# One wait of the store queue, moved up by one store, in a row-sum kernel on one Trainium2 core

## The chip, the core and the metric

The kernel runs on one core of a Trainium2 chip. A core has compute engines that run side by side, each through its own list of instructions in order. Two of them compute here: VectorE (DVE in the profile) and ScalarE (ACT). SyncE (SP, and SPq in the profile for its issuing instructions) computes nothing: it issues all DMA transfers and waits on semaphores between them. The engines meet only through semaphores, which compute instructions raise by 1 and DMA transfers by 16 in all. The metric is the time of one execution on the device in microseconds (us), the median of three runs.

## The reference: what is computed

```python
def setup_inputs():
    batch, seq, dim = 32, 512, 1024
    return {"x": np.random.randn(batch, seq, dim).astype(np.float32)}

def reference(x):
    relu_x = np.maximum(x, 0)
    return np.sum(relu_x, axis=-1).astype(np.float32)
```

Each of the 32 x 512 = 16,384 rows of 1,024 floats is clipped at zero and summed. 67.11 MB are read, 64 KB are written.

## The kernel before

**Tiling.** The rows are dealt to the 128 partitions, 128 rows to each. Of the output they form three regions, `REGIONS = [1, 111, 16]` rows per partition. In the first region, partition p holds row p. In the second, each partition holds 111 rows that follow one another, and in the third 16. The sums are gathered in `res`, 128 partitions by 128 columns, one column for each row of a partition.

**Loads.** Seven chunks of 16 rows per partition (8 MB each) go to three buffers in turn. SP issues them at line 91; from the fourth chunk on it first waits until DVE is done with the buffer (`s_dve`, lines 86 and 87). Then follow, with no wait between them but the one on the first, the loads of the last region: 8, 4 and 2 rows (line 101), and the last two rows in four pieces. Three pieces are issued at line 112, with one semaphore each, `s_in[-3]`, `s_in[-2]` and `s_in[-1]`. The third piece, 256 columns, is the last load but one. The fourth, `seam` (line 115, semaphore `s_seam`), takes the rest, 368 columns across the border between the two rows, and is the last load.

**Compute.** In the first six chunks ACT clips (line 145) and DVE sums (line 160). From the seventh chunk on, each engine clips and sums whole rows by itself, every other one (helpers at lines 127 and 130). Of the last two rows, DVE sums the third piece when `s_in[-1]` is there (lines 197 and 198), and both engines finish on `seam` (lines 201 and 203), which raises `s_last` to 2.

**The first region's sums.** They stand in column 0 of `res`, one float in each partition. After chunk 1, DVE transposes the first 32 columns in blocks of 32 by 32 into `turned` (line 169) and raises `s_turn`. The sums are then in the four partitions 0, 32, 64 and 96, 32 floats (128 bytes) in each.

**Stores.** All three are issued by SP, in this order, after all loads:

1. line 117: the 4 x 128 bytes of `turned`, after a wait for `s_turn` (line 116). This text calls it the turned store.
2. line 123: the second region, 128 partitions x 444 bytes (55.5 KB), after waits for the last sums of that region (`s_fact`, `s_fdve`, lines 120 and 121) and for `s_in[-1]` (line 122). This is the bulk store. Both of these raise `s_store` by 16.
3. line 207: the third region, 128 x 64 bytes (8 KB), after a wait for `s_last` (line 206). This is the final store; it raises `s_out`.

The program ends when `s_store` stands at 32 and `s_out` at 16 (lines 208 and 209). A wait need not become an instruction of its own: one wait rides on the DMA instruction behind it, and others are put together in one wait instruction ahead of it. In the trace, SP has a single wait instruction ahead of the bulk store (for `s_in[-1]` and `s_fdve`, shown as line 122), and the bulk store itself carries the wait for `s_fact`.

Of the kernel before, what the change touches and what calls it, by code (L numbers as in the profile page):

```python
# [16 lines left out]
def bass_relu_sum_kernel(  # L17
# [40 lines left out]
    s_in = [nc.alloc_semaphore(f"s_in{i}") for i in range(n_in)]  # L58
# [11 lines left out]
    sp, act, dve = nc.sync, nc.scalar, nc.vector  # L70
# [40 lines left out]
    for k, (lo, hi) in enumerate((first, second, third)):  # L111
# [2 lines left out]
        )  # L114
    sp.dma_start(out=seam[:, 2 : 2 + w + HEAD], in_=rows[:, CUT : D + HEAD]).then_inc(s_seam, 16)
    sp.wait_ge(s_turn, 1)
    sp.dma_start(
        out=of[0:P].rearrange("(k q) -> k q", q=32), in_=turned[0:P:32, 0:32]
    ).then_inc(s_store, 16)
    sp.wait_ge(s_fact, 1)  # L120
    sp.wait_ge(s_fdve, 1)
    sp.wait_ge(s_in[-1], 16)
    sp.dma_start(out=ov[1][:, :], in_=res[:, start[1] : start[2]]).then_inc(s_store, 16)


# [112 lines left out]
```

## Time and profile before

| | |
|---|---|
| median of 3 runs | 160.82 us (160.79 to 160.82) |
| span of the profiled execution, first to last instruction | 159.4 us (159.394 in the trace) |
| what lies around the span, by the difference to the median | 1.43 us |
| DVE busy | 120.6 us, 76% of the span |
| ACT busy | 101.5 us, 64% of the span |
| DMA queue | 2,456 packets, 67.18 MB, 98.1% of 16 engines' span |
| mean rate of reading HBM | 421 GB/s |

No separate total time is recorded for the profiled execution, so its span stands beside the median of the timed runs. Times below that count from the start of the span are points on the trace's clock.

The profile page gives each engine's busy time, a chain of work that ended last, and groups of instructions with their mean durations. The trace behind it holds every instruction with its start and duration, every DMA packet, and the time of every increment that reached a semaphore. A view of waits tells what an engine waited for, and a view of stretches gives the busy time and the moved bytes between two points.

### The profile page before, as it was taken

What the parts mean: (1) busy time and instruction counts of PE and PEld (TensorE: products, weight loads), DVE (VectorE), ACT (ScalarE), POOL (GpSimd) and SP (SyncE); (2) the same over time, 40 slices, a digit from 0 to 9 for tenths busy, and PEclk for the clock granted to TensorE, in tenths of its full rate; (3) what the DMA queues carried; (4) which work ended last, traced back from release to release, by engine and by line L of the source; (5) the groups of instructions that cost most, each with busy time, mean ns of one, the idle gap of its engine ahead of it and who ended that gap; (6) DMA issues with size and microseconds to landing.
All of it is one profiled execution on the core that took longest, in us unless ns stands there. A gap on an engine that the chain in (4) does not pass through costs nothing.

```text
span 159.4 us, 150 instructions
## 1 busy us (share of the span) xinstructions
DVE 120.6 (76%) x59; ACT 101.5 (64%) x54; POOL 0.2 (0%) x4
## 2 busy tenths in 40 slices
DVE  0000000009999999999999999999999999898995
ACT  3000059980799708996099941999329980496975
POOL 0000000000000000000000000000000000000000
DMA  9997996996996997989979969969969979798994
GB/s 378 493 401 339 493 526 263 526 526 263 526 493 296 526 444 345 526 378 411 526 312 477 526 263 526 526 263 526 526 263 526 444 345 526 321 469 374 417 400 142
DMA packets 2457, 67.18 MB, mean 421 GB/s; under 512 B 536, under 2 KB 792, under 8 KB 1176
## 3 DMA queue, kind: packets, MB, share of 16 engines
q1 hardware_dynamic: 2456, 67.18, 98.1%
q14 instruction: 1, 0.01, 0.0%
HBM read 67.11 MB, written 0.07 MB: 421 GB/s over the span
## 4 chain that ended last, share of the span: by engine, by line
DVE 55%; DMA 34%; ACT 9%; SPq 2%; issue 0%
DVE res L160 54%; DMA buf<-in_x_dram 34%; ACT buf L145 9%; SPq L101 1%; SPq L112 1%; DVE buf L130 0%; DVE seam L130 0%; SPq L91 0%; DVE turned L169 0%
## 5 line engine op out<-in xcount | busy, mean ns | idle before, releaser
L160 DVE TENSOR_REDUCE res<-buf 128x4 f32<-128x4096 f32 (+3 forms) x18 | 99.4, 5596 | 35.5 <-ACT buf L145 35.5
L145 ACT ACTIVATE buf<-buf 128x7168 f32<-128x7168 f32 (+5 forms) x13 | 80.4, 6233 | 46.1 <-DMA buf<-in_x_dram 46.1
L127 ACT ACTIVATE buf<-buf 128x1024 f32<-128x1024 f32 (+2 forms) x19 | 19.0, 999 | 8.9 <-DMA buf<-in_x_dram 8.9
L130 DVE TENSOR_SCALAR_CACHE_REDUCE buf<-buf 128x1024 f32<-128x1024 f32 (+2 forms) x19 | 20.7, 1143 | 1.7 <-DMA buf<-in_x_dram 1.6
L127 ACT ACTIVATION_READ_ACCUMULATOR buf<-buf 128x1 f32 x19 | 3.6, 188 | 0.0
L145 ACT ACT_TABLE_LOAD x1 | 1.3, 1283 | 1.3 <-PEq L223 1.3
L130 DVE DVE_READ_ACCUMULATOR buf<-buf 128x1 f32 x19 | 1.6, 84 | 0.0
L130 DVE TENSOR_SCALAR_CACHE_REDUCE seam<-seam 128x258 f32<-128x258 f32 x1 | 0.4, 421 | 0.0
L127 ACT ACTIVATE seam<-seam 128x114 f32<-128x114 f32 x1 | 0.3, 300 | 0.1
L169 DVE STREAM_TRANSPOSE turned<-res 128x32 f32<-128x32 f32 x1 | 0.2, 211 | 0.0
L127 ACT ACTIVATION_READ_ACCUMULATOR seam<-seam 128x1 f32 x1 | 0.2, 186 | 0.0
L223 POOL MEMSET const-bfloat16-1.0<- 128x1 bf16 x1 | 0.1, 101 | 0.0
L223 POOL MEMSET const-uint8-127<- 128x1 uint8 x1 | 0.1, 101 | 0.0
L223 POOL MEMSET const-float32-0.0<- 128x1 f32 x1 | 0.1, 98 | 0.2 <-issue 0.2
L223 POOL MEMSET const-float32-1.0<- 128x1 f32 x1 | 0.1, 98 | 0.0
L130 DVE DVE_READ_ACCUMULATOR seam<-seam 128x1 f32 x1 | 0.1, 82 | 0.0
## 6 DMA issues: line engine op xcount, KB each, us to landing
buf<-in_x_dram SPq DMA_DIRECT2D x1, 7680.0 KB, 21.1
buf<-in_x_dram SPq DMA_DIRECT2D x1, 4096.0 KB, 25.3
buf<-in_x_dram SPq DMA_DIRECT2D x1, 2048.0 KB, 29.9
buf<-in_x_dram SPq DMA_DIRECT2D x1, 1024.0 KB, 31.9
buf<-in_x_dram SPq DMA_DIRECT2D x1, 512.0 KB, 3.3
buf<-in_x_dram SPq DMA_DIRECT2D x1, 456.0 KB, 32.5
buf<-in_x_dram SPq DMA_DIRECT2D x1, 256.0 KB, 32.7
seam<-in_x_dram SPq DMA_DIRECT2D x1, 184.0 KB, 32.6
```

The costliest lines, as they stand in the source:

```text
L101: sp.dma_start(out=buf[:, tb, r : r + n, :], in_=xv[-1][:, r : r + n, :]).then_inc(s_in[NBIG + i], 16)
L112: sp.dma_start(out=flat[:, lo:hi], in_=rows[:, lo:hi]).then_inc(s_in[NBIG + len(TAIL) + k], 16)
L127: return act.activation(t, t, AF.Relu, accum_out=acc)
L130: return dve.tensor_scalar(out=t, in0=t, scalar1=0.0, scalar2=None, op0=ALU.max, op1=ALU.add, accum_out=acc)
L145: act.activation(t, t, AF.Relu).then_inc(s_act, 1)
L160: dve.tensor_reduce(out=res[:, c * BIG + r : c * BIG + r + n], in_=buf[:, c % NB, r : r + n, :], axis=X, op=ALU.add,).then_inc(s_dve, 1)
L169: dve.transpose(out=turned[:, :], in_=res[:, 0:32]).then_inc(s_turn, 1)
L223: nc = _bacc.Bacc("TRN2", target_bir_lowering=False, num_devices=1)
```

## The change

```diff
     sp.dma_start(out=seam[:, 2 : 2 + w + HEAD], in_=rows[:, CUT : D + HEAD]).then_inc(s_seam, 16)
     sp.wait_ge(s_turn, 1)
+    sp.wait_ge(s_in[-1], 16)
     sp.dma_start(
         out=of[0:P].rearrange("(k q) -> k q", q=32), in_=turned[0:P:32, 0:32]
     ).then_inc(s_store, 16)
     sp.wait_ge(s_fact, 1)
     sp.wait_ge(s_fdve, 1)
-    sp.wait_ge(s_in[-1], 16)
     sp.dma_start(out=ov[1][:, :], in_=res[:, start[1] : start[2]]).then_inc(s_store, 16)
```

The wait for `s_in[-1]` moves from the bulk store to the turned store in front of it. SP issues the same three stores in the same order. The turned store is now issued after the last load but one has landed, and the bulk store is issued after the turned store, its own waits for `s_fact` and `s_fdve` between them. Nothing changes on DVE and ACT, nor in the loads.

## The prediction

> **What bounds the kernel now.** I read the page's head and its chain first, then the end of the chain in order of time, then SP's waits, because the change touches only SP.
>
> ```profile
> span 159.4 us, 150 instructions
> ...
> q1 hardware_dynamic: 2456, 67.18, 98.1%
> ...
> DVE 55%; DMA 34%; ACT 9%; SPq 2%; issue 0%
> ```
>
> The DMA engines are full for 98% of the span: the kernel is bound by reading its input. Nothing in the diff touches that stream until it runs dry, so the question is the last three microseconds. The chain of work in order of time ends so (start, length, what):
>
> ```profile
> 124.39 32.60 DMA buf<-in_x_dram
> 156.99 0.02 issue
> 157.01 0.44 DVE buf L130 x2
> 157.45 0.02 issue
> 157.47 0.43 DVE seam L130 x2
> ```
>
> The third piece of the last rows lands at 156.99 (`s_in[-1]`). DVE sums it, then the seam, and is done at 157.90. The rest is stores. SP's timeline (start, length) and its waits (total, times, longest) show where:
>
> ```profile
> 124.87 0.44 SPq L115 DMA_DIRECT2D seam<-in_x_dram  x1
> 125.35 0.63 SPq L117 DMA_DIRECT2D out_dram<-turned  x1
> 157.08 0.34 SPq L123 DMA_DIRECT2D out_dram<-res  x1
> 157.93 0.34 SPq L207 DMA_DIRECT2D out_dram<-res  x1
> ```
>
> ```profile
> SPq L122 <- DMA buf<-in_x_dram: 31.0, 1, 31.0
> ...
> SPq L209 <- DMA out_dram<-res: 1.1, 1, 1.1
> SPq L207 <- DVE seam L130: 0.5, 1, 0.5
> ```
>
> The turned store's issue stands at 125.35, in a gap of 31 us in which SP has nothing else to do. The bulk store follows 156.99 at once. Then SP idles 0.51 us (157.42 to 157.93) until DVE is done, and issues the final store. It idles 1.1 us more until that lands. So the tail now has two spare places: **0.51 us of SP** between the two stores, and the distance between the bulk store's landing and the final store's. The trace's record of semaphore arrivals gives the second. The bulk store's 16 increments come in two groups, 13 at 158.47 to 158.70 and three stragglers at 159.02, 159.03 and 159.05. The final store's come at 159.17 to 159.35. So the bulk store has **0.30 us** to spare. Counted from the issue's start the bulk store lands after 1.39 to 1.97 us (from 157.08), the final one after 1.24 to 1.42 us (from 157.93). The view of stretches (columns: stretch, length, busy times, clock, DMA share, GB/s) shows the same gap from issue to movement:
>
> ```profile
> 157.00:157.90 0.90, 0.85 (x4) 0.76 (x4) 0.00 (x0) 1.00 0.00 0
> 157.90:158.30 0.40, 0.00 (x1) 0.00 (x0) 0.00 (x0) 1.00 0.50 142
> 158.30:158.75 0.45, 0.00 (x0) 0.00 (x0) 0.00 (x0) 1.00 0.00 0
> 158.75:159.00 0.25, 0.00 (x0) 0.00 (x0) 0.00 (x0) 1.00 0.37 33
> ```
>
> The bulk store's bytes move from 157.92 on, 0.84 us behind its issue, the final store's from 158.76, 0.83 us behind its own, and between them nothing moves.
>
> **The change part by part.**
>
> *Removed: the turned store in the 31 us gap.* Its 0.63 us of issue were hidden there and give back nothing. Its four packets lay behind the loads: by the packet records they ran at 156.53 to 156.63, 13 ns each, and their increments came at 157.15 to 157.32. They stand behind the seam's packets, so I take the gain for the loads as 0. The other bound is in the last rival.
>
> *Added: the turned store between 156.99 and the bulk store.* What it costs SP there isn't in the trace. Its own row says 0.633 us, but that was the last of eight issues in a row. In that row, issues behind another take 0.433 to 0.463 us, and issues after a wait 0.327 to 0.343. The turned store has 0.633 - 0.441 = 0.192 us more than the load just before it. After a wait I therefore take 0.343 + 0.192 = **0.535 us**; bounds 0.34 (an issue like any other after a wait) and 0.63 (its own row).
>
> *Added: one wait instruction.* Before, the two waits that remained ahead of the bulk store rode in one wait instruction and on the store. Now each of the two stores has two waits, so a wait instruction stands between them as well. Both its semaphores were raised by 146.94 (their arrivals), so it costs only its passing: the start of SP's wait instruction to the start of the bulk store was 0.075 us, and one issue's end to the next start 0.042 us, together **0.12 us**; the lower bound is 0.04, if it vanishes.
>
> *Moved: the bulk store.* It starts 0.535 + 0.12 = 0.655 us later, at 157.735 (bounds 0.38 and 0.75 later). Its landing moves with it: 159.05 + 0.655 = 159.705. The 0.30 us to spare are used up and **0.355 us** stay over.
>
> *Moved: the final store.* Queued behind the bulk store on SP. The bulk issue takes 0.343 us (after a wait) to 0.441 us (behind another issue), so SP is free at 158.08 to 158.18 and starts the final store 0.042 us later, at 158.12 to 158.22 instead of 157.93. That is 0.19 to 0.29 us late, and with 1.42 us to landing the end is 159.54 to 159.64. This is less than the 0.355 of the bulk store. The two run side by side, so the larger counts.
>
> *The rest.* The turned store itself lands early enough: with even the bulk store's longest 1.97 us it is there at 159.05. No load, ACT or DVE instruction waits for any of SP's stores.
>
> **The sum**: 159.394 + 0.355 = 159.75 us of span; around it stay 1.43 us, so 160.82 + 0.355 = **161.17 us**, 0.22% more. A change of 0.2%, 0.32 us, is about what a measurement of this kernel can tell from none; the forecast is just beyond it.
>
> *Two rules weighed.* The record of arrivals for the turned store shows five: one at 126.37, 0.39 us behind the end of its issue, and four with its packets. The Trainium skill, DMA: Bandwidth & Descriptors, section on why a DMA increments its semaphore by 16, says that a transfer which uses only k engines has the issuing sequencer write the other 16 - k itself, at once; that fits the 0.192 us more on the issue, and by it that surcharge goes along to the new place. The same page (Rules for kernel authors) says to issue a DMA early so that its fixed cost overlaps, which speaks against this change, and its section on the anatomy of one DMA puts that fixed cost at about 2.0 us (for another issuing path). By that price a bulk store at 157.735 would land at 159.74 and the final store at 160.12, which would make the loss 0.77 us; but the same price makes the final store of before land at 159.93, and its row says 159.35, so the rows decide.
>
> **The rivals.**
>
> 1. *The stragglers don't come again.* If the three late arrivals of the bulk store belong to that one execution, its landing is 158.70 + 0.655 = 159.36 and the final store decides: +0.19 to +0.29, so 161.01 to 161.11 us, within 0.2%. For it: 13 of 16 arrivals come 0.3 us sooner. Against it: the bulk store's 128 packets of 444 bytes are the same after the change.
> 2. *The spare SP time swallows nearly all* (the side of not slower). Place: the 0.51 us of SP before the final store; price: if the turned store costs only 0.34 + 0.04 us after a wait, the bulk store starts at 157.46, its issue ends at 157.80, and the final store stays at 157.93. The bulk landing is 159.43, +0.08, so 160.90 us. It decides as long as the bulk store is delayed less than 0.47 us (0.51 less one gap), for then the final store doesn't move. For it: after waits all of SP's issues fall to 0.33 to 0.34. Against it: the 0.192 us surcharge over a load beside it.
> 3. *SP is held until the early increment has arrived.* That was 1.02 us behind the start of the issue (126.37 against 125.35). No DMA was issued behind it before, so the trace can't exclude it. Then the bulk store starts at about 157.08 + 1.02 + 0.08 = 158.18, 1.10 us later, and lands at 160.15: +0.80, 161.62 us. Against it: SP's wait instruction counts its 31.0 us from 125.99, the end of the issue.
> 4. *The loads gain by the store's removal.* In the last 3 us of loading (154 to 157) the rates are 391, 383 and 265 GB/s in the three stretches of 1 us, 1.04 MB; at the mean 421 GB/s that takes 2.47 us instead of 2.96, so 0.49 us is the most that undisturbed reads could give. With rival 2's +0.08 that is 160.41 us; it becomes faster than 0.2% only if both hold. Against it: the four packets ran at 156.53, after 2.5 of those 3 us.
>
> **How the numbers follow.** Forecast 0.46: its range 161.05 to 161.30, of which 0.38 lies beyond 161.14. Rival 1: 0.20. Rival 2: 0.11. Rival 3: 0.16. Rival 4: 0.07. Slower by over 0.2%: 0.38 + 0.16 = 0.54. Within 0.2%: 0.08 + 0.20 + 0.11 = 0.39. Faster: 0.07. The range takes in rivals 1 and 2 at the low end (160.88) and the larger part of rival 3's way at the high end (161.55). What it leaves out is rival 4 and the end of rival 3.
>
> **What would show it.** In the changed profile: L117 (one line lower) starts at about 157.08 and takes 0.53 us; a wait instruction and the bulk store's issue follow at 157.7; the final store's issue starts at 158.1 to 158.2 without a wait for DVE ahead of it; the chain ends through SP, not DVE; the bulk store's last increment comes at 159.7, at or behind the final store's. `s_in[-1]` still lands at 156.99. I'm wrong in the first step if the turned issue takes 0.34 or over 0.7 us, in the second if the bulk arrivals have no stragglers, and altogether if the last load lands earlier or later by more than 0.1 us.

## The result and the profile after

The changed kernel takes **162.29 us** (162.19 to 162.33), the kernel before 160.82 (160.79 to 160.87): a ratio of **1.0089**, 95% interval 1.0077 to 1.0101. It is slower by 1.47 us, as forecast in sign, but four times the forecast 0.35, and outside the range. The span grew by more, 1.57 us (159.39 to 160.96): around it lie 1.37 us here, where the prediction took 1.43 from a median and a span of different executions.

The profiled execution took 162.33 us, 160.96 us of it span. The head of the page after:

```profile
span 161.0 us, 151 instructions
...
DVE 120.6 (75%) x59; ACT 101.5 (63%) x54; POOL 0.2 (0%) x4
...
q1 hardware_dynamic: 2456, 67.18, 97.1%
q14 instruction: 1, 0.01, 0.0%
```

The engines' work is the same to a tenth. SP has one instruction more. SP's waits after (total, times, longest) and its timeline in the tail:

```profile
SPq L117 <- DMA buf<-in_x_dram: 31.7, 1, 31.7
...
SPq L209 <- DMA out_dram<-res: 2.2, 1, 2.2
```

```profile
157.15 0.63 SPq L118 DMA_DIRECT2D out_dram<-turned  x1
157.89 0.35 SPq L123 DMA_DIRECT2D out_dram<-res  x1
158.29 0.42 SPq L207 DMA_DIRECT2D out_dram<-res  x1
```

The 0.5 us wait for DVE ahead of the final store is gone, as said, and the final store is issued 0.36 us later. But the last wait is 2.2 us instead of 1.1. The issues' view of the same kernel (size, us from issue to landing) gives for the final store

```profile
out_dram<-res SPq DMA_DIRECT2D x1, 8.0 KB, 2.6
```

where the kernel before has

```profile
out_dram<-res SPq DMA_DIRECT2D x1, 8.0 KB, 1.4
```

This is the row that the prediction didn't see coming: the same 8 KB take 1.2 us longer to land. The view of stretches, after (stretch, length, busy times, clock, DMA share, GB/s), shows when they move:

```profile
159.20:159.42 0.22, 0.00 (x0) 0.00 (x0) 0.00 (x0) 1.00 0.39 35
159.42:159.57 0.15, 0.00 (x0) 0.00 (x0) 0.00 (x0) 1.00 0.00 0
159.57:159.94 0.37, 0.00 (x0) 0.00 (x0) 0.00 (x0) 1.00 0.07 24
159.94:160.90 0.96, 0.00 (x0) 0.00 (x0) 0.00 (x0) 1.00 0.00 0
```

The final store's packets run from 159.21, and 120 of its 128 are through at 159.41. Then something runs from 159.57 to 159.94 that fills only 0.07 of the engines, one of 16, at 24 GB/s. The packet records name it: one packet of 8,192 bytes on **queue 14**, the `q14 instruction` of the page, from 159.571 to 159.878; and behind it, from 159.875 to 159.924 (their starts), the last eight of the final store's packets, as many as one DMA engine's share. What kept them from 159.21 until the fetch's packet began, at 159.571, stands in no record. Fifteen of the final store's increments had come by 160.04. The sixteenth came at **160.92**, and the span ends on it. Before, this same instruction fetch stood behind all stores (final store's packets, nothing, the fetch):

```profile
158.76:158.97 0.21, 0.00 (x0) 0.00 (x0) 0.00 (x0) 1.00 0.44 39
158.97:159.21 0.24, 0.00 (x0) 0.00 (x0) 0.00 (x0) 1.00 0.00 0
159.21:159.39 0.18, 0.00 (x0) 0.00 (x0) 0.00 (x0) 1.00 0.17 46
```

### The profile page after: what moved, and what is told of

It is laid out like the page before. It is cut to its first block, busy times and chain, and to the rows that moved or that the text cites. A ratio compares the mean times of both kernels' runs of the same rounds, so it can differ in the third digit from the quotient of the medians.

```text
span 161.0 us, 151 instructions
## 1 busy us (share of the span) xinstructions
DVE 120.6 (75%) x59; ACT 101.5 (63%) x54; POOL 0.2 (0%) x4
## 4 chain that ended last, share of the span: by engine, by line
DVE 54%; DMA 33%; ACT 9%; SPq 2%; issue 0%
DVE res L160 54%; DMA buf<-in_x_dram 33%; ACT buf L145 9%; SPq L101 1%; SPq L112 1%; DVE buf L130 0%; DVE seam L130 0%; SPq L91 0%; DVE turned L169 0%
## 6 DMA issues: line engine op xcount, KB each, us to landing
buf<-in_x_dram SPq DMA_DIRECT2D x1, 456.0 KB, 32.6
seam<-in_x_dram SPq DMA_DIRECT2D x1, 184.0 KB, 32.6
```

## The experiments

**The theories.** A: the final store, now late, meets the instruction fetch; one DMA engine carries its share behind the fetch, and that increment, alone 0.88 us behind the others, is most of the loss. The variants of A differ in what sets off the fetch. B: the writes of three stores in flight hold each other up, and the fetch is incidental. C: it needs the turned store's four packets or its issue.

### Seven runs that repeated the two kernels

I wanted to move the fetch by lengthening one engine's instruction stream with no-operations, 64 of them or one, and in e11 to delay the final store with 18:

```diff
+    for _ in range(64):
+        nc.vector.nop(nofuse=True)   # DVE; in other runs SP, ACT, POOL, PE
     k = 0
     for c in range(NTWO):
```

The traces don't have the no-operations: each engine has as many instructions there as without them, and in e11 the final store is issued at 158.286, where the changed kernel has 158.293. I take it that they never reached the chip. So these runs tell nothing of what they were made for, and are repeats: six of the changed kernel, one of the kernel before.

> The changed kernel with 64 no-operation instructions on SP in its idle 31 us, ahead of the turned store's waits. Theory A (the 8 KB instruction fetch seen at 159.571, on queue 14, holds up one DMA engine's share of the final store; it comes when SP reaches a certain place in its instruction stream): the no-operations move the fetch away from the tail, the last increment at 160.92 goes, the rest ends as the other 15 do at 160.04, so 161.4 us. Theory B (the final store is late because three stores' writes are in flight together; the fetch only happens to be there): 162.3 us.

> The kernel before with a single no-operation on SP in the idle 31 us, so that its stream has as many instructions as the changed kernel's. Theory A, if the place is a count of instructions: the fetch comes one instruction sooner and can meet the final store, up to 161.9 us. Theory A, if the fetch is tied to the final store's own issue, and theory B: 160.8 us.

> The changed kernel with 64 no-operations at the head of DVE's stream, where DVE idles until 35 us. The no-operations on SP left the fetch where it was, so SP's stream isn't what fetches. Theory A2 (the fetch belongs to the stream of another engine that comes to its end at about 157.9): on the engine that owns it the no-operations move it out of the tail, and the time falls to 161.2 to 161.5 us; on the other engines nothing moves, 162.3. DVE is my first guess. Theory B (stores' writes hold each other up): 162.3 us on all four engines.

> The same on ACT, which idles until 21 us. Theory A2: 161.2 to 161.5 us if the fetch is ACT's, my second guess, 162.3 otherwise. Theory B: 162.3 us.

> The same on GpSimd (POOL), which has nothing to do after its four memsets. Theory A2: 162.3 us, since its stream comes to its end early, unless it waits for the others at the end and fetches there: then 161.2 to 161.5. Theory B: 162.3 us.

> The same on TensorE (PE), which has nothing to do in this kernel. Theory A2: 162.3 us, since its stream comes to its end early, unless it waits for the others at the end and fetches there: then 161.2 to 161.5. Theory B: 162.3 us.

> The changed kernel with 18 no-operations on SP ahead of the final store's wait, so that it is issued later still, by some 0.3 to 0.9 us (what a no-operation costs on SP isn't known from the runs so far). Theory A: packets that come after the fetch has ended (159.9) aren't held up, so the time hardly rises or falls in spite of the delay: 161.8 to 162.4 us, and the 16 increments come close together. Theory B and a plain delay: 162.3 plus the whole delay, 162.6 to 163.2.

Measured: 162.35, 162.23, 162.30, 162.32, 162.32 and 162.32 us for the six (in the order above without the second), and 160.81 us for e2. As repeats they show that the picture is no accident. In all six profiles the last of the final store's packets starts 0.045 or 0.046 us after the fetch's packet has ended, and one increment is alone, 0.89 to 1.14 us behind the other fifteen. In e2, as before, the packets are through ahead of the fetch.

### e3, e4 and e10: is it the turned store, or the lateness?

e3 issues the bulk store first and the turned store between it and the final one:

```diff
-    sp.wait_ge(s_turn, 1)
-    sp.dma_start(... in_=turned[0:P:32, 0:32]).then_inc(s_store, 16)
     sp.wait_ge(s_fact, 1)
     sp.wait_ge(s_fdve, 1)
     sp.wait_ge(s_in[-1], 16)
     sp.dma_start(out=ov[1][:, :], in_=res[:, start[1] : start[2]]).then_inc(s_store, 16)
+    sp.wait_ge(s_turn, 1)
+    sp.dma_start(... in_=turned[0:P:32, 0:32]).then_inc(s_store, 16)
```

> The order bulk store (with the wait for the last load but one), turned store, final store; SP has as many instructions as before. The bulk store stays at 157.08, the final store is issued behind the turned store at about 158.1. Theory A: its packets come later after its issue than behind a wait (0.92 us instead of 0.83) and can meet the fetch, 162.0 us or, where the fetch stays behind, 161.0. Theory B: three stores in flight, 162.0 us. My prediction's account, in which stores only queue on SP: 161.0 us.

e4 is the changed kernel with one semaphore for the two waits ahead of the bulk store, so that the wait instruction between the stores goes:

```diff
-    sp.wait_ge(s_fact, 1)
-    sp.wait_ge(s_fdve, 1)
+    sp.wait_ge(s_fact, 2)
```

> The changed kernel with one semaphore in place of s_fact and s_fdve, so that the wait instruction between the turned and the bulk store goes and SP has as many instructions as before. Theory A, if the place is a count of instructions: the fetch comes one instruction later and misses the final store, 161.3 us. Theory A tied to the final store's issue: 162.2 us. Theory B: 162.2 us (0.05 less for the wait instruction).

e10 is the kernel before, the turned store early, with another wait ahead of the bulk store:

```diff
-    sp.wait_ge(s_in[-1], 16)
+    sp.wait_ge(s_last, 2)
     sp.dma_start(out=ov[1][:, :], in_=res[:, start[1] : start[2]]).then_inc(s_store, 16)
```

> The kernel before, the turned store early as it was; the bulk store waits for s_last instead of the last load but one, so that bulk and final store are issued one behind the other from 157.93 and the final store at about 158.31. Theory A: its packets run at 159.2 and one engine's share meets the fetch, 162.2 us. Theory C (it needs the turned store in the tail, its four packets or its longer issue): 161.2 us. Theory B: between them, two stores in flight instead of three, 161.3 to 161.8.

Measured: e3 162.09, e4 162.35, e10 162.19 us (ratio of e10 to before 1.0083, 1.0068 to 1.0098). SP's timeline of e10 and the landing of its final store:

```profile
158.18 0.34 SPq L123 DMA_DIRECT2D out_dram<-res  x1
158.56 0.43 SPq L207 DMA_DIRECT2D out_dram<-res  x1
```

```profile
out_dram<-res SPq DMA_DIRECT2D x1, 8.0 KB, 2.2
```

In e10 no turned store is near; its packets are there at 156.5, with the loads. Still one increment of the final store comes alone, at 160.76, the others by 160.17, and the fetch lies at 159.414 to 159.776. So C falls: **a late final store is enough**. e3 says the same with the bulk store at its old place (fetch 159.343 to 159.723, last increment 160.69; its time fits A and B alike). e4 shows that the number of SP's instructions doesn't set off the fetch: with one less, it comes at 159.570, against 159.571.

### e13 and e9: moving the fetch by an engine's end

In both, the changed kernel gets one op more on one engine, behind its last sum, into a spare cell; no store waits for it. e13 on ACT, e9 on DVE:

```diff
     on_dve(seam[:, k : k + HEAD + 2], res[:, J - 1 : J]).then_inc(s_last, 1)
+    on_act(flat[:, D + D // 2 : 2 * D], spare[:, 1:2])    # e13
+    on_dve(flat[:, CUT // 2 : CUT], spare[:, 0:1])        # e9, instead
```

> The same with ACT in place of DVE: one op more (512 elements) after its last sum, so that only ACT's end comes 0.8 us later. Theory A3: 161.3 us if the fetch is ACT's, otherwise 162.3. Theory B: 162.3 us.

> The changed kernel; DVE does one op more (456 elements of a piece that is already summed, into a spare cell) after its last sum has raised s_last, so that only DVE's end comes 0.7 us later. No store waits for it. Theory A3 (the fetch comes at the end of one engine's own work, about 1.3 to 1.5 us behind it): if the engine is DVE, the fetch moves to about 160.2, behind the final store's packets, and the time falls to 161.3 us; if not, 162.3. Theory B (stores' writes hold each other up): 162.3 us.

Measured: **e13 161.33 us** (ratio to before 1.0032, 1.0021 to 1.0044), as the theory had it for the owner of the fetch; **e9 161.90 us** (1.0069, 1.0054 to 1.0084), neither of its two numbers. A useless op on ACT takes 0.96 us off the changed kernel. The stretches and the final store's row of e13 show why:

```profile
159.20:159.42 0.22, 0.00 (x0) 0.00 (x0) 0.00 (x0) 1.00 0.34 29
159.42:159.85 0.43, 0.00 (x0) 0.00 (x0) 0.00 (x0) 1.00 0.00 0
159.85:159.93 0.08, 0.00 (x0) 0.00 (x0) 0.00 (x0) 1.00 0.59 102
```

```profile
out_dram<-res SPq DMA_DIRECT2D x1, 8.0 KB, 1.6
```

The three stores are issued at 157.11, 157.85 and 158.24, within 0.05 us of the changed kernel's, with the same writes in flight. But the fetch now comes at 159.857, behind the final store's packets (159.161 to 159.359), and all 16 increments are there by 159.89. **So B falls, and the collision's price is 0.96 us** (1.03 us of span). e13 also has a second fetch, at 161.228, behind the span; with ACT's two instructions more it may be ACT's, but no run tells. Of all eighteen profiles, ten have the final store's lone late increment, and in these ten and no others its last eight packets start at the fetch's end, 3 to 4 ns ahead of it.

In e9 there is no fetch in the tail either, and the final store's increments stay together. But the fetch has moved the other way, to 151.616 among the loads, and the last load but one lands at 157.64, its other fifteen increments by 157.09. The same holds for every load that lands behind the fetch, there and in e18 below: one increment comes 0.54 to 0.66 us behind the others, where the loads ahead of the fetch have at most 0.1.

### e15, e16, e18: whose fetch it is

e15 (on the changed kernel) and e16 (on the one before) sum pieces that are ready together in one op, five DVE instructions fewer for the same work:

```diff
-DVE_STEPS = [[4, 5, 7], [7, 4, 5], [7, 4, 5], [7, 4, 5], [4, 5, 7], [3, 4, 5]]
+DVE_STEPS = [[16], [7, 9], [7, 9], [7, 9], [4, 5, 7], [3, 4, 5]]
```

e18 is e9's op on the kernel before.

> The changed kernel with five instructions fewer on DVE: in the first four chunks, pieces that are ready at the same time are summed in one op instead of two or three. Theory A4 (the fetch is DVE's, and comes when DVE's stream reaches a certain count just behind its last sum, past the wait at the program's end): with five instructions fewer that count is reached only after the stores have landed, no fetch lies in the span, and the time is 161.2 to 161.4 us. If the fetch is ACT's or anyone else's, and theory B (the stores hold each other up): 162.2 to 162.3 us.

> The same five instructions fewer in the kernel before. Theory A4: no fetch in the span, but there it was behind the final store's packets and cost nothing, 160.7 to 160.85 us. If the fetch also made the three late increments of the bulk store, these go, without effect on the end.

> The kernel before with one DVE op more behind its last sum (nothing waits for it). Theory A4: as in the changed kernel with this op, the fetch comes at about 151.6 among the loads, one DMA engine's share of every later load comes about 0.5 us late, and the time is 161.3 to 161.5 us. If that late load in the changed kernel was chance, 160.8 us.

Measured: e15 161.80 us (1.0057, 1.0042 to 1.0072), e16 161.33 us (1.0032, 1.0019 to 1.0045), e18 161.47 us (1.0038, 1.0023 to 1.0053). The queues on the page of e15:

```profile
q1 hardware_dynamic: 2456, 67.18, 97.7%
HBM read 67.11 MB, written 0.07 MB: 420 GB/s over the span
```

The line for q14 is gone: no fetch in the span, which falls to 159.93 us, 1.03 less than after. That is the expected mechanism. The expected time isn't met, in e15 nor in e16: the fetch still comes, at 161.608 and 161.145, behind the span, in what the program does after its last instruction, and that is longer. Between total and span of the same execution lie 1.85 us in e15 (161.78 - 159.93) and 1.89 in e16 (161.34 - 159.45), against 1.37 in the changed kernel. e16's span is as before, 159.45. That the fetch makes this half microsecond is argued from its place, not shown: in both runs the semaphore signals of the program's end stand still 0.42 us longer than elsewhere, but they go on 0.31 and 0.35 us before the fetch's packet has ended, and e13, which has a packet of that kind behind its span too, has 1.49.

e18 met its range. The fetch is at 151.707, and the end of its chain of waits (start, length, what) and the row of the last load but one (us to landing) read:

```profile
124.48 33.24 DMA buf<-in_x_dram
157.73 0.02 issue
```

```profile
buf<-in_x_dram SPq DMA_DIRECT2D x1, 128.0 KB, 33.2
```

against 32.60 and 32.6 before. Fifteen of its increments are there by 157.16, the last at 157.73: one engine is late, and every sum behind it. So adding DVE instructions, before or after, draws the fetch forward by over seven microseconds, and removing them pushes it back by two, while ACT's two in e13 move it by 0.29: **its place goes by DVE's instructions**, so I take the fetch for DVE's. That ACT's op also moved it, while DVE's own end stayed, fits a wait of DVE for ACT at the program's end: a semaphore that the kernel doesn't use is raised there three times, the last at 158.06 before and at 158.70 in e13, and the fetch follows 1.15 and 1.16 us behind. It isn't a fixed distance: in the changed kernel the fetch comes 1.43 us behind (158.14), and 1.18 to 1.47 in the other nine runs where it meets the final store. This link is argued, not shown; e13 met its number, while e9, on the engine that I take for the owner, missed. Why two instructions more move the fetch by seven microseconds stays open.

### e17: a shorter way to the final store

The changed kernel, with the first region's sums stored from 128 partitions, 4 bytes each:

```diff
     sp.dma_start(
-        out=of[0:P].rearrange("(k q) -> k q", q=32), in_=turned[0:P:32, 0:32]
+        out=ov[0][:, :], in_=res[:, 0:1]
     ).then_inc(s_store, 16)
```

> The changed kernel; the first region's sums are stored from all 128 partitions, 4 bytes each out of res, in place of 128 bytes from each of four. Its issue should take 0.34 to 0.44 us instead of 0.63, so the final store is issued at about 158.0 to 158.1 and its packets run from 158.9 to 159.1. Theory A: if they are through before the fetch at 159.2, 160.95 to 161.1 us; if some are not, 162.0. Theory B: 161.9 us or more, 128 more small writes being in flight.

Measured: 167.68 us (1.0429, 1.0412 to 1.0445). The issue took 0.343 us, the final store's issue started at 157.96, and its packets ran from 158.89 to 159.10, ahead of the fetch (159.345), all about as expected. The time was missed by over 6 us. The landings of the three stores (bulk, turned, final):

```profile
out_dram<-res SPq DMA_DIRECT2D x1, 55.5 KB, 8.3
out_dram<-res SPq DMA_DIRECT2D x1, 0.5 KB, 5.9
out_dram<-res SPq DMA_DIRECT2D x1, 8.0 KB, 8.2
```

512 bytes in writes of 4 take 5.9 us to land and hold up the stores behind them to 8 us, although the last packet of all three is through at 159.10. (The first two raise one semaphore; the view gives its first sixteen increments to the first, so 5.9 us is the least.) The run can't tell how much lateness the collision needs; it says what the transpose on DVE is there for.

No version beat the kernel before. Its fetch has the best place that the runs show.

## Why the prediction was wrong

**Right: the removal.** Nothing was gained at 125 us, and the loads gained nothing, though the turned store's packets had run among the seam's (to 156.97) and not behind them: the last load but one landed at 157.07, against 156.99. Rival 4 falls.

**Right in kind, too small: the turned store's issue.** 0.632 us after a wait, not 0.535. It is its own row of before, the upper bound. e17's 0.343 for the same place with 128 partitions shows the surcharge: 0.29, not 0.192. The increment that came ahead of the packets is there again 1.01 us behind the issue's start (158.16); SP wasn't held until it, so rival 3 falls.

**Right: the wait instruction and SP's queue.** From the end of the turned issue to the bulk's start 0.108 us (forecast 0.12); the bulk's issue took 0.349; the final issue started 0.36 us later than before, of which 0.08 is the loads' later end. The forecast was 0.19 to 0.29.

**Wrong: which store lands last.** The bulk store's three stragglers didn't come again. Its last increment came at 159.53, 1.64 us behind its start, not 1.97. This was rival 1, and with it the final store decides. e2, the repeat of the kernel before, has no stragglers either: its bulk store is there at 158.72, 0.65 us ahead of the final store's 159.37. So the 0.30 us to spare, on which the forecast's 0.355 stands, was a reading of one execution. In e13 six of the bulk's increments come in a late group again, at 159.58 to 159.67, so the stragglers come and go; what makes them stays open.

**The step that failed: "Moved: the final store", with "1.42 us to landing".** I carried the landing time along as a constant of the transfer. It was 2.62 us (158.293 to 160.917). e13 splits the difference. Without the collision the final store is issued 0.31 us later than before (158.24) and takes 1.65 us to land, 0.23 more than before: 0.54 us of span, where I had given this path 0.19 to 0.29 and the bulk store's 0.355. By the medians, e13 is 0.50 us over before. Of the 0.23 us, 0.09 are there when the first packet moves (0.92 us behind the issue's start, before 0.83); why the landing takes longer in the denser queue, no run shows, but e9 and e15, which have no collision either, take 1.62. The other **0.96 us** (162.29 - 161.33) is a collision that the prediction didn't name. The fetch's packet was in the trace of before, at 159.212 to 159.705. I read the semaphore arrivals and the store packets up to it, and took the rest of the span and what lies around it as fixed. Moving the final store's packets by 0.44 us (158.765 to 159.208) put them where the fetch was on its way: by the 1.15 us of before it would have begun at about 159.29 (an estimate, 158.14 + 1.15), amid the packets of 159.21 to 159.41. It began at 159.57, which fits that each held up the other.

**Two sentences of the Trainium skill, beside this.** DMA: Bandwidth & Descriptors, section Queues, rings and completion order, says that a semaphore increment lands only after every earlier write of its DMA engine, whatever the queue. That would have the late increment wait for the fetch's own write; here it came 0.99 us behind its own record (159.931 to 160.92), while the other fifteen, paired in order of time, took 0.36 to 0.65. In the other nine such runs it came 0.74 to 0.93 us behind its record. That fits, but no run shows the cause. Runtime: NRT & Kernel Launch, section Instruction fetch mechanics, calls the cost of a crossing to the next block of instructions mostly hidden. Here it cost nothing visible where it came behind the final store's packets, in the kernel before and in e13; it cost 0.96 us on the final store and 0.62 us among the loads (e18, 161.47 against 160.85), and where it came behind the end the time was 0.48 us longer (e16, 161.33 against 160.85), so the measurements decide.

## What to carry to other kernels

A store at the end of a kernel has a neighbour that no line of the code shows: read the packet records to the last one, every queue, and ask for each packet near the end what happens if your transfer comes half a microsecond later. A transfer's time to landing isn't a constant that can be carried along; one late increment of sixteen is enough to end the program later. And a wait that makes small work late has its price in what is queued behind it, not in the work itself: the turned store itself landed by 158.76, two microseconds ahead of the end.

## What the runs showed of the hardware

- An instruction fetch of 8 KB, a packet of 0.3 to 0.8 us (2.7 in e17), cost between nothing and 1 us, by where it fell. One DVE op more or five fewer moved it by microseconds, so a change of the instruction count alone can go with half a microsecond: e16 does the work of the kernel before in five instructions less and is 0.48 us slower.
- A store of 4 x 128 bytes from four partitions takes SP 0.63 us to issue, wherever it stands; one over 128 partitions takes 0.34 in the same place.
- 128 writes of 4 bytes to HBM take at least 5.9 us to land (e17) and slow the stores behind them from 1.6 to over 8 us; 128 writes of 64 bytes take 1.4.
